# A seven-product step for three of eight k pairs in the last two gate chunks, with sums of weights built in place

## The chip, the cores and the metric

The kernel runs on one core of a Trainium2 chip. The metric is the device time of one execution in microseconds (us). Each time below that has a colon in its window is counted from the start of the profiled execution.

## What is computed

One layer of a hybrid trunk on 256 tokens, width 2048, in float32. The parts that matter here:

```python
gates = sigmoid(h @ w_gate + b_gate).reshape(b, s, 3, d)      # w_gate: 2048 x 6144
merged = gates[:, :, 0] * ya + gates[:, :, 1] * yb + gates[:, :, 2] * yc
x = x + merged @ w_o                                          # 2048 x 2048
h2 = rmsnorm(x, g_mlp)
x = x + square(relu(h2 @ w_up)) @ w_down                      # 2048 x 8192, 8192 x 2048
```

Before that stand an input projection and three short token mixers that give ya, yb and yc; after it a last RMSNorm.

## The kernel before, in words

**Products.** Every weight matrix is read once, in slabs of 1 MB (a tile `raw` of 128 x 2048 values). To keep float32's accuracy with TensorE's float32r operands, each operand is split in a high part and a rest: ScalarE (ACT) writes `hi`, a rounding cast of `raw`, and VectorE (DVE) writes `lo = raw - hi`. One product of a 128 x 128 block of activations with a 128 x 512 block of weights is then three matmuls of 512 columns into one accumulator in PSUM: act_hi by hi, act_hi by lo, act_lo by hi.

**Weights in the pipeline.** Class `W` (lines 75 to 121) loads a slab and prepares it. `raw` has three buffers, `hi` and `lo` two each. `next_w` keeps the preparation of one slab ahead of the matmuls of another: slab p is cast into the `hi` buffer that slab p-2 had, so its cast waits until PE has done the last matmul that reads slab p-2.

**Stages.** Up to 197 us the input projection and the mixers. Then six gate chunks of 1024 columns in the order of `BRANCH_TURNS`, each of eight slabs (two k tiles of 128 by 1024 columns, "one k pair"), each followed by its branch's projection of two or three slabs (`gate`, `branch`, lines 526 to 552). Then the output projection, and four rounds q of an up projection (16 slabs) and a down projection of two chunks c (8 slabs each).

**The seven-product step.** `down_folded` (line 644) already uses it, for seven of the eight down chunks. A slab of two k tiles, two token tiles and two column blocks takes 8 products, 24 matmuls. In the four k pairs of `FOLD` it takes 7 products, 21 matmuls: four sums of activations (`sact`) are made once a round, and four sums of weight blocks for each slab (`W.sums`, line 105). The sums go through a tile `t` of their own: three DVE additions into `t` (lines 110 to 112), then casts `th` and rests `tl` in two halves (lines 116 and 117), then `hi` and `lo` of the three raw blocks that are used as they are (the same lines, 128 x 1536). `th` and `tl` have one buffer. Some products go to one output alone (`dx`), four are shared between outputs and gather in `mb` and `ma`.

```python
nc.vector.tensor_add(t[:, 0:2, :], v[:, 0:3:2, :], v[:, 3:4, :].to_broadcast([P, 2, 512]))
nc.vector.tensor_add(t[:, 2, :], t[:, 1, :], v[:, 0, :])
nc.vector.tensor_add(t[:, 3, :], t[:, 2, :], v[:, 1, :])
```

**Order.** Each engine works through its own list in the order that a scheduler wrote when the program was built, and waits at an instruction until semaphores of the other engines allow it. Within a chunk the scheduler may move matmuls among neighbours.

Names used below: slabs are numbered as they are loaded. Slabs 126 to 133 are the first down chunk of the first round (127, 129, 131, 133 folded), 134 to 141 the second. A sum's tiles bear the number of the slab plus one (`th132` belongs to slab 131).

Of the kernel before, what the change touches and what calls it, by code (L numbers as in the profile page):

```python
# [25 lines left out]
FOLD = (1, 3, 5, 7)  # L26
BRANCH_TURNS = ((2, 0, NCB), (1, 0, NB), (2, 1, NCB), (1, 1, NB), (0, 0, NA), (0, 1, NA))
# [19 lines left out]
def hybrid_trunk(ctx: ExitStack, tc: tile.TileContext, xw_d, gmix_d, xtok_d, wst, wtok, wbr, par_d, wpool_d, bgate_d, gfin_d, out_d):  # L47
# [37 lines left out]
    class W:  # L85
# [19 lines left out]
        def sums(self):  # L105
            v, hi, lo = four(self.raw), four(self.hi), four(self.lo)
            t = pools["fold"].tile([P, 4, 512], F32, name=f"t{serial[0]}", tag="t")
            self.thi = pools["fold"].tile([P, 4, 512], F32R, name=f"th{serial[0]}", tag="th")
            self.tlo = pools["fold"].tile([P, 4, 512], F32R, name=f"tl{serial[0]}", tag="tl")
            nc.vector.tensor_add(t[:, 0:2, :], v[:, 0:3:2, :], v[:, 3:4, :].to_broadcast([P, 2, 512]))  # L110
            nc.vector.tensor_add(t[:, 2, :], t[:, 1, :], v[:, 0, :])
            nc.vector.tensor_add(t[:, 3, :], t[:, 2, :], v[:, 1, :])
            for h, l, r in ((self.thi[:, 0:2, :], self.tlo[:, 0:2, :], t[:, 0:2, :]),
                            (self.thi[:, 2:4, :], self.tlo[:, 2:4, :], t[:, 2:4, :]),
                            (hi[:, 0:3, :], lo[:, 0:3, :], v[:, 0:3, :])):
                fg[1] = nc.scalar.copy(h, r)  # L116
                fg[0] = nc.vector.tensor_sub(l, r, h.bitcast(F32))  # L117
# [398 lines left out]


# [3 lines left out]
    gt = gstack.enter_context(tc.tile_pool(name="gt", bufs=2))  # L521
    acc = gp.tile([P, 2, D], F32, name="acc")
    mstack = ExitStack()
    home = [None]
# [16 lines left out]
    def branch(c, ks, gs, name, n, first=False):  # L541
        banks = fresh_banks(1024, name)
        gemm_tok(yact, banks, 1024, ks, n=n)
        for h in range(2):
# [9 lines left out]
    def merged_channels(c):  # L554
        tp = ps_pair(f"tm{c}").rearrange("p a b -> p (a b)").rearrange("p (j s) -> p j s", s=S)
# [4 lines left out]
        split(home[0][:, 4 * c:4 * c + 4, :], tp)  # L560

    SPAN = {2: list(range(NA + NB, KT)), 1: list(range(NA, NA + NB)), 0: list(range(NA))}
    for b, c, nk in BRANCH_TURNS:
        if b == 0 and c == 0:
# [3 lines left out]
            mp = mstack.enter_context(tc.tile_pool(name="mp", bufs=1, side="right"))  # L568
            home[0] = mp.tile([P, KT, 2 * S], F32R, name="merged")
        turn = {1: lambda: merged_channels(0), 2: lambda: merged_channels(1)} if (b, c) == (0, 1) else None  # L570
        gs = gate(b, c, 4, turn)
        branch(c, SPAN[b], gs, f"y{b}_{c}", 4, first=b == 2)
    merged = home[0]
# [298 lines left out]
```

## Time and profile before

| | |
|---|---|
| median of three runs | 1347.83 us (1347.45 to 1348.12) |
| the profiled execution | 1347.23 us |
| its span, first to last instruction | 1345.3 us |
| PE busy | 1332.8 us, 99% of the span |
| DVE busy | 1009.5 us, 75% |
| ACT busy | 657.6 us, 49% |
| HBM read | 264.71 MB, 198 GB/s over the span |

The profile is of one execution on the chip. Its page gives busy time by engine, the span in 40 slices, and groups of instructions by source line; the trace behind it can be asked for the instructions of a stretch in order of time (a timeline), for busy times in chosen stretches, and for what ended an engine's idle time. Busy time of PE counts overlapping matmuls once, so PE can read as busy all the time; the rate at which matmuls start tells how fast it goes.

### The profile page before, as it was taken

How to read it: one execution, taken by the hardware profiler on the slowest of the kernel's cores; microseconds unless marked ns; L12 is line 12 of the kernel's file. 1: busy time of each engine (PE TensorE's matmuls, PEld its weight loads, DVE VectorE, ACT ScalarE, POOL GpSimd, SP SyncE). 2: the span in 40 equal slices, each digit the busy share in tenths (PEclk: the TensorE clock that was granted, in tenths of full speed). 3: DMA queues.
4: the chain of work that ended last, by engine and by line, in shares of the span. 5: the costliest groups of instructions: out<-in, count | busy, mean ns of one | idle time of the engine just before them, and what ended most of it. 6: DMA issues, size and time to landing. Idle time of an engine off the chain costs nothing.

```text
span 1345.3 us, 16492 instructions
## 1 busy us (share of the span) xinstructions
PE 1332.8 (99%) x6610; PEld 1127.1 (84%) x6610; DVE 1009.5 (75%) x1267; ACT 657.6 (49%) x796; POOL 21.7 (2%) x47
## 2 busy tenths in 40 slices
PE   9999999999999999999999999999999999999997
PEld 8888888888888888888888888888788888888885
DVE  6779888879766465555668996679876799777966
ACT  7545443434454344345445564455544455444544
POOL 0000000000000000000000000000110001100010
PEclk9999999999999999999999999999999999999999
DMA  9655555656556565565455555555775557755682
GB/s 372 221 188 188 188 188 191 211 201 210 197 185 208 197 212 176 197 241 188 157 191 199 204 204 202 188 189 190 227 239 184 192 199 222 236 189 188 214 255 94
DMA packets 42557, 273.11 MB, mean 203 GB/s; under 512 B 4848, under 2 KB 4976, under 8 KB 11888
## 3 DMA queue, kind: packets, MB, share of 16 engines
q1 hardware_dynamic: 38736, 263.67, 56.2%
q0 software_dynamic: 2880, 5.24, 2.2%
q10 hardware_dynamic: 864, 3.15, 0.6%
q8 instruction: 51, 0.84, 0.2%
q14 instruction: 26, 0.21, 0.0%
HBM read 264.71 MB, written 2.10 MB: 198 GB/s over the span
## 4 chain that ended last, share of the span: by engine, by line
PE 91%; DVE 4%; DMA 3%; issue 1%; ACT 0%; SPq 0%; POOLq 0%; POOL 0%; DVEq 0%; ACTq 0%
PE u L124 17%; PE u L127 9%; PE g L511 6%; PE g L510 6%; PE g L512 6%; PE dx L641 4%; PE dx L640 4%; PE dx L642 4%; PE zc L124 3%; PE o L511 2%; PE o L510 2%; PE o L512 2%; PE za L124 2%; DMA raw<-wtok 2%; PE y L511 2%; PE y L510 2%
## 5 line engine op out<-in xcount | busy, mean ns | idle before, releaser
L120 ACT CAST hi<-raw 128x1024 fp32r<-128x1024 f32 x420 | 423.6, 1050 | 434.6 <-PE g L512 134.4
L121 DVE TENSOR_TENSOR lo<-raw,hi 128x1024 fp32r<-128x1024 f32 x420 | 502.0, 1220 | 178.4 <-ACT hi L120 178.3
L124 PE MATMUL u<-hact,hi 128*128 128x512 f32 x1024 | 245.4, 391 | 0.0
L124 PEld LDWEIGHTS u<-hact,hi 128*128 128x128 f32 x1024 | 187.8, 188 | 36.9 <-ACT ps L685 0.4
L510 PE MATMUL g<-hi,hact 128*128 128x512 f32 x384 | 149.9, 390 | 0.0
L512 PE MATMUL g<-hi,hact 128*128 128x512 f32 x384 | 149.4, 389 | 0.0
L511 PE MATMUL g<-lo,hact 128*128 128x512 f32 x384 | 149.4, 389 | 0.0
L127 PEld LDWEIGHTS u<-hact,lo 128*128 128x128 f32 x1024 | 131.4, 191 | 5.1
L127 PE MATMUL u<-hact,lo 128*128 128x256 f32 x1024 | 133.0, 283 | 0.0
L641 PE MATMUL dx<-lo,yact 128*128 128x512 f32 x252 | 98.8, 392 | 0.2 <-DVE lo L121 0.2
L640 PE MATMUL dx<-hi,yact 128*128 128x512 f32 x252 | 98.8, 392 | 0.0
L642 PE MATMUL dx<-hi,yact 128*128 128x512 f32 x252 | 98.4, 391 | 0.0
L329 DVE SCALAR_TENSOR_TENSOR va<-upad,par,va 128x256 f32<-128x256 f32 x180 | 86.8, 482 | 3.4
L510 PEld LDWEIGHTS g<-hi,hact 128*128 128x128 f32 x384 | 72.1, 188 | 15.0
L512 PEld LDWEIGHTS g<-hi,hact 128*128 128x128 f32 x384 | 72.1, 188 | 15.0
L511 PEld LDWEIGHTS g<-lo,hact 128*128 128x128 f32 x384 | 72.1, 188 | 14.8
L116 ACT CAST th<-t 128x1024 fp32r<-128x1024 f32 x56 | 57.5, 1052 | 33.9 <-PE dx L642 15.9
L117 DVE TENSOR_TENSOR tl<-t,th 128x1024 fp32r<-128x1024 f32 x56 | 67.0, 1221 | 8.1 <-ACT th L116 8.1
L192 DVE TENSOR_TENSOR zs_u<-u,cr_u 128x512 f32<-128x512 f32 x32 | 22.1, 692 | 60.6 <-ACT cr_u L190 60.6
L190 ACT COPY cr_u<-u 128x512 f32<-128x512 f32 x32 | 18.8, 588 | 90.6 <-PE u L124 83.4
L640 PEld LDWEIGHTS dx<-hi,yact 128*128 128x128 f32 x252 | 47.3, 188 | 11.4 <-ACT ps L685 0.4
L641 PEld LDWEIGHTS dx<-lo,yact 128*128 128x128 f32 x252 | 47.3, 188 | 10.4 <-DVE lo L121 0.6
(213 smaller groups left out, 1893.1 us busy)
## 6 DMA issues: line engine op xcount, KB each, us to landing
raw<-wtok SPq DMA_DIRECT2D x128, 1024.0 KB, 4.9
raw<-wst SPq DMA_DIRECT2D x93, 1024.0 KB, 4.9
raw<-wbr SPq DMA_DIRECT2D x16, 1024.0 KB, 4.8
xw<-xw SPq DMA_DIRECT2D x7, 768.0 KB, 8.4
macc<-ps POOLq DMA_DIRECT2D x20, 256.0 KB, 7.5
bias<-bgate SPq DMA_DIRECT2D x6, 512.0 KB, 3.6
xt<-xtok SPq DMA_DIRECT2D x8, 256.0 KB, 9.0
xres<-xtok ACTq DMA_DIRECT2D x1, 2048.0 KB, 9.2
```

What stands on the lines that cost most here:

```text
L117: fg[0] = nc.vector.tensor_sub(l, r, h.bitcast(F32))
L120: fg[1] = nc.scalar.copy(self.hi[:, ks], self.raw[:, ks])
L121: fg[0] = nc.vector.tensor_sub(self.lo[:, ks], self.raw[:, ks], self.hi[:, ks].bitcast(F32))
L124: nc.tensor.matmul(ps, w.hi[:, k, :], act[:, ak, :], start=start, stop=stop)
L127: nc.tensor.matmul(ps[:, S:2 * S], w.lo[:, k, :], act[:, ak, 0:S], start=False, stop=False)
L329: nc.vector.scalar_tensor_tensor(va[:, i, :], upad[:, i, k:k + S], pcol(C_WDW + i * KA + k), va[:, i, :], ALU.mult, ALU.add)
L510: nc.tensor.matmul(banks[t][:, c, :], left, hi[:, i, cols], start=first, stop=False)
L511: nc.tensor.matmul(banks[t][:, c, :], left, lo[:, i, cols], start=False, stop=False)
L512: nc.tensor.matmul(banks[t][:, c, :], rest, hi[:, i, cols], start=False, stop=last)
L640: nc.tensor.matmul(ps, left[0], right[0], start=start, stop=False)
L641: nc.tensor.matmul(ps, left[0], right[1], start=False, stop=False)
L642: nc.tensor.matmul(ps, left[1], right[0], start=False, stop=stop)
```

## The change

Four things change together.

1. The gate chunks of branch 0 (the last two, `gate_folded`) use the seven-product step in k pairs 3, 5 and 7 (`GFOLD`). Their activation sums `gsact` are made during an earlier gate chunk. The shared products are taken apart after the chunk, partly beside the branch's matmuls.
2. `W.sums`, for gates and down chunks alike, drops the tile `t`. It first casts `hi` and takes `lo` of three raw blocks, then adds in place over `raw`, then casts `th` and takes `tl`.
3. The merged activations lie in two tiles of half the size. The transposes of the first two quarters use the PSUM tiles `mb` and `ma` of the second folded gate chunk, ahead of their products.
4. The order of the blocks in a folded slab and of its products is another, and `gfin` has a tile of its own.

```diff
+GFOLD = (3, 5, 7)
...
         def sums(self):
             v, hi, lo = four(self.raw), four(self.hi), four(self.lo)
-            t = pools["fold"].tile([P, 4, 512], F32, name=f"t{serial[0]}", tag="t")
...
-            nc.vector.tensor_add(t[:, 0:2, :], v[:, 0:3:2, :], v[:, 3:4, :].to_broadcast([P, 2, 512]))
-            nc.vector.tensor_add(t[:, 2, :], t[:, 1, :], v[:, 0, :])
-            nc.vector.tensor_add(t[:, 3, :], t[:, 2, :], v[:, 1, :])
-            for h, l, r in ((self.thi[:, 0:2, :], self.tlo[:, 0:2, :], t[:, 0:2, :]),
-                            (self.thi[:, 2:4, :], self.tlo[:, 2:4, :], t[:, 2:4, :]),
-                            (hi[:, 0:3, :], lo[:, 0:3, :], v[:, 0:3, :])):
-                fg[1] = nc.scalar.copy(h, r)
-                fg[0] = nc.vector.tensor_sub(l, r, h.bitcast(F32))
+            fg[1] = nc.scalar.copy(hi[:, 0:3, :], v[:, 0:3, :])
+            nc.vector.tensor_sub(lo[:, 0:3, :], v[:, 0:3, :], hi[:, 0:3, :].bitcast(F32))
+            nc.vector.tensor_add(v[:, 0:4:3, :], v[:, 0:2, :], v[:, 3:4, :].to_broadcast([P, 2, 512]))
+            nc.vector.tensor_add(v[:, 1, :], v[:, 1, :], v[:, 0, :])
+            nc.vector.tensor_add(v[:, 2, :], v[:, 2, :], v[:, 1, :])
+            for ks in (slice(0, 4, 3), slice(1, 3)):
+                fg[1] = nc.scalar.copy(self.thi[:, ks, :], v[:, ks, :])
+                fg[0] = nc.vector.tensor_sub(self.tlo[:, ks, :], v[:, ks, :], self.thi[:, ks, :].bitcast(F32))
...
-        stream += [(wtok[next(tok)], KT) for i in range(8)]
+        stream += [(wtok[next(tok)], KT, 1, turn[0] == 0 and i in GFOLD) for i in range(8)]
...
+    def folded_products(av, sums, pairs, name, between=None):
...
+                own = [(xs[0][:, 0, :], a12, b21), (xs[0][:, 1, :], s4, b22), (xs[1][:, 0, :], a22, t4)]
+                shared = [(mb[:, 1, :], s1, t1), (mb[:, 0, :], s3, t3), (ma[:, 1, :], s2, t2), (ma[:, 0, :], a11, b11)]
+                if last:
+                    for ps, left, right in own:
+                        mm3(ps, left, right, False, True)
+                for ps, left, right in shared:
+                    mm3(ps, left, right, first, last)
+                if not last:
+                    for ps, left, right in own:
+                        mm3(ps, left, right)
...
+    def gate_folded(c, between):
...
+        xs, mb, ma = folded_products(hact, gsact, GFOLD, f"g{c}", between)
...
+        for t in range(2):
+            nc.scalar.copy(gs[t], xs[t])
...
+        nc.scalar.copy(m5, mb[:, 1, :])
+        nc.scalar.copy(p1, ma[:, 0, :])
+        def out(t, h, m):
+            g = gs[t][:, h, :]
+            nc.vector.tensor_add(g, g, m)
+            nc.vector.scalar_tensor_tensor(g, g, rtok[:, t:t + 1], bias[:, 512 * h:512 * h + 512], ALU.mult, ALU.add)
+            nc.scalar.activation(g, g, AF.Sigmoid)
+        bg.extend([lambda: nc.vector.tensor_sub(u, p1, ma[:, 1, :]), lambda: nc.vector.tensor_sub(v, u, mb[:, 0, :]),
+                   lambda: out(0, 0, p1), lambda: nc.vector.tensor_sub(u, m5, u), lambda: out(1, 0, v),
+                   lambda: out(0, 1, u), lambda: nc.vector.tensor_sub(v, m5, v), lambda: out(1, 1, v)])
...
+    def gate_sums(i):
+        k = 2 * GFOLD[i]
+        whole = tmp.tile([P, 2, S], F32, name=f"whole{i}", tag="mg")
+        nc.vector.tensor_add(whole, hact[:, k:k + 2, 0:S].bitcast(F32), hact[:, k:k + 2, S:2 * S].bitcast(F32))
...
     for b, c, nk in BRANCH_TURNS:
+        if b == 1 and c == 1:
+            bg.extend([lambda i=i: gate_sums(i) for i in range(len(GFOLD))])
...
-        gs = gate(b, c, 4, turn)
-        branch(c, SPAN[b], gs, f"y{b}_{c}", 4, first=b == 2)
+        gs = gate_folded(c, turn_merged if c else None) if b == 0 else gate(b, c, 4)
+        branch(c, SPAN[b], gs, f"y{b}_{c}", 4, first=b == 2, b0=b == 0)
```

The built program of the changed kernel shows how the lists of the engines come to stand. Three places:

**First place: DVE, preparation of slab 131** (folded; slabs 130 and 132 beside it are plain). Before:

```order
L110 TENSOR_TENSOR t132_5831<-raw131_5827 128x1024 [waits DMAHW7_49,DVE_49]
L111 TENSOR_TENSOR t132_5831<-t132_5831,raw131_5827 128x512 [waits DVE_49]
L112 TENSOR_TENSOR t132_5831<-t132_5831,raw131_5827 128x512 [waits DVE_49]
L121 TENSOR_TENSOR lo130_5800<-raw130_5798,hi130_5799 128x1024 [waits DMAHW6_49,Activation_49]
L121 TENSOR_TENSOR lo130_5800<-raw130_5798,hi130_5799 128x1024 [waits Activation_49]
L117 TENSOR_TENSOR tl132_5833<-t132_5831,th132_5832 128x1024 [waits Activation_49] x2
L117 TENSOR_TENSOR lo131_5829<-raw131_5827,hi131_5828 128x1536 [waits Activation_49]
```

With the change:

```order
L111 TENSOR_TENSOR lo131_5922<-raw131_5920,hi131_5921 128x1536 [waits DMAHW0_49,Activation_49]
L112 TENSOR_TENSOR raw131_5920<-raw131_5920 128x2x512 [waits DVE_49]
L121 TENSOR_TENSOR lo132_5961<-raw132_5959,hi132_5960 128x1024 [waits DMAHW1_49,Activation_49]
L113 TENSOR_TENSOR raw131_5920<-raw131_5920 128x512 [waits DVE_49]
L121 TENSOR_TENSOR lo132_5961<-raw132_5959,hi132_5960 128x1024 [waits Activation_49]
L114 TENSOR_TENSOR raw131_5920<-raw131_5920 128x512 [waits DVE_49]
L117 TENSOR_TENSOR tl132_5925<-raw131_5920,th132_5924 128x2x512 [waits Activation_49]
L117 TENSOR_TENSOR tl132_5925<-raw131_5920,th132_5924 128x1024 [waits Activation_49]
```

Before, the sums come first, as soon as the load has landed, and `lo` last. With the change `lo` comes first, the sums wait for it, and both halves of the next plain slab's `lo` (132, where it was 130's) stand among the additions and ahead of `tl`.

**The same place on ACT.** Before:

```order
L120 CAST hi130_5799<-raw130_5798 128x1024 [waits DMAHW6_49,PE_49,Activation_49]
L120 CAST hi130_5799<-raw130_5798 128x1024
L116 CAST th132_5832<-t132_5831 128x1024 [waits DVE_49,PE_49,Activation_49]
L116 CAST th132_5832<-t132_5831 128x1024 [waits DVE_49]
L116 CAST hi131_5828<-raw131_5827 128x1536 [waits DMAHW7_49,PE_49]
```

With the change:

```order
L110 CAST hi131_5921<-raw131_5920 128x1536 [waits DMAHW0_49,PE_49,Activation_49]
L120 CAST hi132_5960<-raw132_5959 128x1024 [waits DMAHW1_49,PE_49,Activation_49]
L120 CAST hi132_5960<-raw132_5959 128x1024
L116 CAST th132_5924<-raw131_5920 128x2x512 [waits DVE_49,Activation_49]
L116 CAST th132_5924<-raw131_5920 128x1024 [waits DVE_49]
```

The cast of the folded slab's own blocks has moved from last to first, and the two casts of the next plain slab 132 stand ahead of both casts of sums.

**Second place: PE, folded slab 131.** Before, from the last matmul of slab 130:

```order
L642 MATMUL dx0_0_1_5686<-hi130_5799,yact_89 128x512
L640 MATMUL mb0_0_5687<-th132_5832,sact_4920 128x512 [waits Activation_49]
L641 MATMUL mb0_0_5687<-tl132_5833,sact_4920 128x512 [waits DVE_49]
L642 MATMUL mb0_0_5687<-th132_5832,sact_4920 128x512
L640 MATMUL mb0_0_5687<-th132_5832,sact_4920 128x512
L641 MATMUL mb0_0_5687<-tl132_5833,sact_4920 128x512
L642 MATMUL mb0_0_5687<-th132_5832,sact_4920 128x512
L640 MATMUL ma0_0_5688<-th132_5832,sact_4920 128x512 [waits Activation_49]
L641 MATMUL ma0_0_5688<-tl132_5833,sact_4920 128x512 [waits DVE_49]
L642 MATMUL ma0_0_5688<-th132_5832,sact_4920 128x512
L640 MATMUL ma0_0_5688<-hi131_5828,yact_89 128x512 [waits Activation_49]
L641 MATMUL ma0_0_5688<-lo131_5829,yact_89 128x512 [waits DVE_49]
```

With the change, from the fifth matmul of slab 131:

```order
L519 MATMUL dx0_0_0_5780<-lo131_5922,sact_5015 128x512
L520 MATMUL dx0_0_0_5780<-hi131_5921,sact_5015 128x512
L518 MATMUL dx0_0_0_5780<-hi132_5960,yact_89 128x512 [waits Activation_49]
L519 MATMUL dx0_0_0_5780<-lo132_5961,yact_89 128x512 [waits DVE_49]
L520 MATMUL dx0_0_0_5780<-hi132_5960,yact_89 128x512
L518 MATMUL dx0_0_0_5780<-hi132_5960,yact_89 128x512
L518 MATMUL mb0_0_5782<-th132_5924,sact_5015 128x512 [waits Activation_49]
L519 MATMUL dx0_0_0_5780<-lo132_5961,yact_89 128x512
L520 MATMUL dx0_0_0_5780<-hi132_5960,yact_89 128x512
L518 MATMUL dx0_0_0_5780<-hi132_5960,yact_89 128x512
L519 MATMUL dx0_0_0_5780<-lo132_5961,yact_89 128x512 [waits DVE_49]
L520 MATMUL dx0_0_0_5780<-hi132_5960,yact_89 128x512
```

Before, slab 131 runs as a block, sums first. With the change the products of slab 131's own blocks come first, and then matmuls of slab 132 stand among those of slab 131, each new operand with a wait.

**Third place: PE, the last folded slab of the chunk, 133.** Before, from the last matmul of slab 132:

```order
L642 MATMUL dx0_0_1_5686<-hi132_5868,yact_89 128x512
L640 MATMUL dx0_0_1_5686<-th134_5901,yact_89 128x512 [waits Activation_49]
L641 MATMUL dx0_0_1_5686<-tl134_5902,yact_89 128x512 [waits DVE_49]
L642 MATMUL dx0_0_1_5686<-th134_5901,yact_89 128x512
L640 MATMUL dx0_0_0_5685<-hi133_5897,yact_89 128x512 [waits Activation_49]
L641 MATMUL dx0_0_0_5685<-lo133_5898,yact_89 128x512 [waits DVE_49]
```

With the change, from the fifth matmul of slab 133:

```order
L519 MATMUL dx0_0_0_5780<-lo133_5990,sact_5015 128x512
L520 MATMUL dx0_0_0_5780<-hi133_5989,sact_5015 128x512
L518 MATMUL mb0_0_5782<-th134_5992,sact_5015 128x512 [waits Activation_49]
L518 MATMUL dx0_0_1_5781<-th134_5992,yact_89 128x512 [waits Activation_49]
L519 MATMUL mb0_0_5782<-tl134_5993,sact_5015 128x512 [waits DVE_49]
L520 MATMUL mb0_0_5782<-th134_5992,sact_5015 128x512
L518 MATMUL mb0_0_5782<-th134_5992,sact_5015 128x512
L519 MATMUL mb0_0_5782<-tl134_5993,sact_5015 128x512
L520 MATMUL mb0_0_5782<-th134_5992,sact_5015 128x512
L518 MATMUL ma0_0_5783<-th134_5992,sact_5015 128x512
L519 MATMUL dx0_0_1_5781<-tl134_5993,yact_89 128x512 [waits DVE_49]
```

Before, slab 133 begins with a sum's product. With the change, two matmuls that read the two halves of `th134` stand behind six matmuls of the slab's own blocks, with nothing of another slab between them.

In the second chunk of each round and in the two gate chunks the lists read differently in one respect: ACT casts the first half of the sums ahead of the next plain slab's first half, and DVE makes all three additions and the first `tl` ahead of the next plain slab's `lo`. The order of three additions behind `lo` is the same in all 34 folded slabs (28 in down chunks, 6 in gates).

## Rows read from the trace of the kernel before

**Rows 1.** The page: busy time and instructions; DMA issues, KB each, us to landing
```profile
PE 1332.8 (99%) x6610; PEld 1127.1 (84%) x6610; DVE 1009.5 (75%) x1267; ACT 657.6 (49%) x796; POOL 21.7 (2%) x47
...
raw<-wtok SPq DMA_DIRECT2D x128, 1024.0 KB, 4.9
```

**Rows 2.** Busy time of each engine (and instructions) in four stretches, us from the start
```profile
core 0: us, PE busy (x) PEld busy (x) DVE busy (x) ACT busy (x) POOL busy (x), PEclk, DMA share, GB/s
448.00:476.00 28.00, 28.00 (x125) 23.21 (x124) 14.46 (x14) 12.20 (x14) 0.00 (x0) 1.00 0.61 207
733.00:775.00 42.00, 42.00 (x184) 34.12 (x183) 39.56 (x43) 23.09 (x24) 0.00 (x0) 1.00 0.58 200
1326.00:1330.00 4.00, 3.63 (x15) 2.34 (x13) 2.23 (x3) 0.00 (x0) 0.00 (x0) 1.00 0.00 0
1336.00:1345.00 9.00, 0.31 (x2) 0.00 (x0) 2.55 (x6) 2.06 (x4) 0.55 (x1) 0.70 0.44 164
```

**Rows 3.** Groups by line and shape: count, busy us, mean ns, idle before
```profile
L121 DVE TENSOR_TENSOR lo<-raw,hi 128x1024 fp32r<-128x1024 f32 x420 | 502.0, 1220 | 178.4 <-ACT hi L120 178.3
L120 ACT CAST hi<-raw 128x1024 fp32r<-128x1024 f32 x420 | 423.6, 1050 | 434.6 <-PE g L512 134.4 <-issue 113.5 <-PE dx L642 70.4
...
L117 DVE TENSOR_TENSOR tl<-t,th 128x1024 fp32r<-128x1024 f32 x56 | 67.0, 1221 | 8.1 <-ACT th L116 8.1
L116 ACT CAST th<-t 128x1024 fp32r<-128x1024 f32 x56 | 57.5, 1052 | 33.9 <-PE dx L642 15.9 <-issue 13.5 <-DVE t L112 4.5
...
L117 DVE TENSOR_TENSOR lo<-raw,hi 128x1536 fp32r<-128x1536 f32 x28 | 49.2, 1757 | 2.1 <-ACT hi L116 2.1
...
L116 ACT CAST hi<-raw 128x1536 fp32r<-128x1536 f32 x28 | 41.5, 1482 | 2.4 <-PE dx L642 2.4
```

**Rows 4.** PE's timeline, first and 97th matmul of the gate stage: start, length
```profile
197.64 0.39 PE L510 MATMUL g<-hi,hact 128*128 128x512 f32 x1
...
219.41 0.39 PE L510 MATMUL g<-hi,hact 128*128 128x512 f32 x1
```

**Rows 5.** PE's timeline in folded slab 131 of the first down chunk
```profile
759.69 0.40 PE L642 MATMUL mb<-th,sact 128*128 128x512 f32 x1
...
762.48 0.39 PE L642 MATMUL dx<-th,yact 128*128 128x512 f32 x1
...
763.88 0.39 PE L642 MATMUL dx<-hi,sact 128*128 128x512 f32 x1
```

**Rows 6.** ACT's timeline while slabs 131 and 132 run
```profile
762.95 2.00 ACT L116 CAST th<-t 128x1024 fp32r<-128x1024 f32 x2 [1.51 <-issue]
764.85 1.48 ACT L116 CAST hi<-raw 128x1536 fp32r<-128x1536 f32 x1
```

**Rows 7.** DVE's timeline in the same stretch
```profile
764.03 2.36 DVE L117 TENSOR_TENSOR tl<-t,th 128x1024 fp32r<-128x1024 f32 x2 [1.16 <-ACT th L116]
766.36 1.76 DVE L117 TENSOR_TENSOR lo<-raw,hi 128x1536 fp32r<-128x1536 f32 x1
768.04 1.22 DVE L110 TENSOR_TENSOR t<-raw 128x1024 f32<-128x1024 f32 x1
769.29 0.69 DVE L111 TENSOR_TENSOR t<-t,raw 128x512 f32<-128x512 f32 x1
770.02 0.69 DVE L112 TENSOR_TENSOR t<-t,raw 128x512 f32<-128x512 f32 x1
770.63 0.74 DVE L727 SCALAR_TENSOR_TENSOR xres<-dx,stat,xres 128x512 f32<-128x512 f32 x1
```

**Rows 8.** PE's timeline where folded slab 133 begins
```profile
769.82 0.39 PE L641 MATMUL dx<-tl,yact 128*128 128x512 f32 x1
...
770.51 0.39 PE L641 MATMUL dx<-lo,yact 128*128 128x512 f32 x1
```

**Rows 9.** PE's timeline in the last chunk, round its longest wait
```profile
1329.30 0.39 PE L512 MATMUL d<-hi,yact 128*128 128x512 f32 x1
1330.54 0.50 PE L510 MATMUL d<-hi,yact 128*128 128x512 f32 x1 [0.84 <-DVE xres L727]
```

More of the change, by code (lines that the diff above doesn't have):

```diff
@@ L515, in gemm_tok, with mm3, act @@
             pump(n)
+    def mm3(ps, left, right, start=False, stop=False):
+        nc.tensor.matmul(ps, left[0], right[0], start=start, stop=False)
+        nc.tensor.matmul(ps, left[0], right[1], start=False, stop=False)
+        nc.tensor.matmul(ps, left[1], right[0], start=False, stop=stop)
+    def folded_products(av, sums, pairs, name, between=None):
+        xs = [ps_pair(f"dx{name}_{t}") for t in range(2)]
+        mb, ma = ps_pair(f"mb{name}"), ps_pair(f"ma{name}")
+        def act(k, t):
+            return av[:, k, t * P:(t + 1) * P], av[:, k, S + t * P:S + (t + 1) * P]
+        for p in range(8):
+            w = next_w()
+            hi, lo = four(w.hi), four(w.lo)
+            if p in pairs:
+                i = pairs.index(p)
+                a11, a12, a22 = act(2 * p, 0), act(2 * p + 1, 0), act(2 * p + 1, 1)
+                s1, s2, s3, s4 = ((sums[:, i, 0, n, :], sums[:, i, 1, n, :]) for n in range(4))
+                b11, b22, b21 = ((hi[:, n, :], lo[:, n, :]) for n in range(3))
+                t1, t2, t4, t3 = ((w.thi[:, n, :], w.tlo[:, n, :]) for n in range(4))
+                first, last = i == 0, i == len(pairs) - 1
+                own = [(xs[0][:, 0, :], a12, b21), (xs[0][:, 1, :], s4, b22), (xs[1][:, 0, :], a22, t4)]
[8 more added lines that the diff above has]
+                        mm3(ps, left, right)
+            else:
+                for k in range(2):
+                    for t in range(2):
+                        for h in range(2):
+                            mm3(xs[t][:, h, :], act(2 * p + k, t), (hi[:, 2 * k + h, :], lo[:, 2 * k + h, :]),
+                                p == 0 and k == 0, p == pairs[-1] - 1 and k == 1 and t == h == 1)
+            if between:
+                between(p, mb, ma)
+        return xs, mb, ma
@@ L539, in gate, with branch @@
         return gs
-    def branch(c, ks, gs, name, n, first=False):
+    def branch(c, ks, gs, name, n, first=False, b0=False):
         banks = fresh_banks(1024, name)
         gemm_tok(yact, banks, 1024, ks, n=n)
+        if b0:
+            pump(len(bg))
         for h in range(2):
@@ L835 @@
     for b, c, nk in BRANCH_TURNS:
[L836 removed]
+        wtok += slabs(w_gate[:, b * D + 1024 * c:b * D + 1024 * c + 1024], (1024,), GFOLD if b == 0 else ())
         wbr += slabs(w_out[b][:, 1024 * c:1024 * c + 1024], (1024,))
```

97 lines of the change are left out of this document (41 added, 56 removed).

## The prediction

> **What bounds the kernel now.** I read the page first. PE is busy 99% of the span, DVE 75% [rows 1]. Busy time says little of pace, so I then took PE's timeline: from its first to its 97th matmul of the gate stage 21.77 us pass, 96 steps of 0.2268 us each [rows 4]. In folded slab 131 the 18 steps from 759.69 to 763.88 take 4.19 us, 0.2328 each [rows 5]. PE goes without a pause through gates and down chunks: where no matmul waits, time is the number of matmuls times these steps. Next the busy times by stretch. In the gates DVE works 14.46 of 28 us, in the first down chunk 39.56 of 42 us, while PE starts 184 matmuls, 0.228 us each [rows 2]. So DVE there is nearly as full as PE, and what keeps PE from waiting is that DVE works ahead. How far ahead, the timelines tell: the rests of the sums `tl` of slab 133 start at 764.03 and are both done at 766.39; `lo` follows at 766.36 and is done at 768.12 [rows 7]. PE's first matmul on `tl` of slab 133 starts at 769.82, the first on its `lo` at 770.51 [rows 8]. That lead, 3.4 and 2.4 us, is what the change spends.
>
> **What it saves.** Each of six folded gate slabs loses 3 matmuls: 18 x 0.2268 = 4.1 us. The 126 matmuls that stay in them step at 0.2328 instead of 0.2268: 0.8 us back. **Saved: 3.3 us.**
>
> **What the new order of the sums costs.** Durations [rows 3]: a cast of 1024 takes 1.05 us, of 1536 1.48; a DVE rest of 1024 takes 1.22, of 1536 1.76. Steps [rows 6, 7]: an ACT cast starts 0.95 after the one before; a DVE instruction of 1024 lets the next start 1.14 later, one of 512 0.61 (770.02 to 770.63), and an addition that needs the one before starts 1.25 after one of 1024 and 0.73 after one of 512. Hand-over: the last matmul on `th` of slab 131 starts at 762.48 and takes 0.39, and the next `th` cast starts at 762.95 [rows 5, 6], so 0.47 after a matmul's start; DVE starts at 764.03, 0.03 after that cast's end [rows 6, 7], and I take 0.03 for every other hand-over. In-place additions on two far blocks aren't in this trace. They have the size of line 110's (1.22 at 768.04); two additions of 512 would take 1.38 [rows 7]. I take 1.22; the difference is 0.16 a slab, 5 us at most in all 34.
>
> Before, the additions needed only the load, and ran before PE let go of any buffer. Now they stand behind `lo`, `lo` behind `hi`, and `hi` behind PE's last matmul on slab p-2. I walk through **slab 131 of a first chunk**, in the order shown, with time 0 where the last matmul of slab 130 starts.
> - `hi131` needs the last matmul on `hi129`, 15 steps of 0.23 earlier: it starts at -2.98 and ends at -1.50. `lo131` runs -1.47 to 0.29, the first addition 0.32 to 1.54.
> - `hi132` needs slab 130 done: its halves run 0.47 to 1.52 and 1.42 to 2.47. DVE's order then gives `lo132` first half 1.55 to 2.77, second addition 2.69, `lo132` second half 3.30 to 4.52, third addition 4.44 to 5.13.
> - The first `th` ends at 3.42, the second (it needs the third addition) at 6.21; `tl` ends at 6.27 and 7.46.
> - PE: the 8th matmul (the first on `lo132`) could start at 1.84 and gets its operand at 2.80: 0.96 lost. The 15th (second half of `lo132`) loses 0.14, the 20th (second `th`) 0.54. The others find theirs ready. **1.64 us lost**, and since all starts from what PE frees, no lead builds up: slab 129 is alike.
> - First folded slab of the chunk (127): between `lo` and the additions stand the split and sums of the last activations; the same walk gives 1.2 before the first `th` and 0.8 before the second: 2.0.
> - **Last folded slab (133)**: the same chain, but only six matmuls stand before the first `th` (could start at 1.61, ready 3.45: 1.84 lost) and one more before the second (3.68, ready 6.24: 2.56 lost). A DVE addition to `xres` delays the second `tl` to 8.08, 0.26 more. 4.66 together.
>
> A first chunk loses 2.0 + 2 x 1.64 + 4.66 = 9.9 us; there are four: **39.8 us**.
>
> **Second chunks**: ACT casts `th` before the next `hi`, and DVE adds all three before the next `lo`. The `hi` cast starts 21 steps before time 0, at -4.36; `lo` ends at -1.09, the additions at 1.61, the first `th` at 1.24, the next slab's `hi` at 2.19, the first `tl` at 2.75. The 5th, 8th and 9th matmul wait 0.12, 0.26 and 0.33: 0.7 us. The last folded slab has its first `tl` in the 8th place (0.94) and the second in the 15th (0.67): 1.6. The first, behind a first chunk's end, loses 1.6 by the same steps. 4.6 a chunk, three of them: **13.9 us**.
>
> **Gate chunks** have the order of second chunks: 0.7 and 1.6 for their second and third folded slab. The first: 0.2 in one chunk; in the other two rests of 1.22 for the merged halves stand between `lo` and the additions, 1.1. At each branch's end some 20 DVE instructions of 0.7 us (taking the products apart, gates, `acc`) and 6 rests meet in three slabs, 21 us of work in 16.3 of PE, so the next slab's `lo` is some 0.8 late. Sum 2.5 + 3.4 + 1.6: **7.5 us**.
>
> **What I cost at nothing.** The activations' sums for the gates (some 18 short DVE instructions) run in a gate chunk where DVE is half idle [rows 2]; without that cover, some 8 us. The copies of PSUM on ACT, 1.05 each, end before the branch's first matmuls need the banks by the same walk (5.1 against 6.7). The transposes are as many as before. SP's list is as long, but a folded slab's `raw` is free only after its last `tl`: 7.46 in the walk. The load takes 4.9 [rows 1], and the slab that gets this buffer is cast some 13 us later or more in first chunks; in second ones a plain slab needs it by 11.5 and it was freed at 5.03, 1.5 us to spare.
>
> **Sum**: -3.3 + 39.8 + 13.9 + 7.5 = +57.9. The profiled execution took 1347.2, 1.9 more than its span and 0.6 under the median of the runs: **1405**.
>
> **Rivals.**
> - *Faster: the waits don't come.* Then 3.3 us remain: 1344. It needs operands ready in the order in which the scheduler set PE's list: the chain would have to be shorter by 2.6 us before the last folded slab of a first chunk and by about 1 elsewhere, so it decides at the hand-over of the `hi` buffer; if `hi` didn't wait for PE, DVE's 9.3 us of work would fit the 10.4 of a pair. For it: DVE is idle for part of each pair. Against: `hi` has two buffers. If waits of about 3 us remained, gain and loss would cancel, to within 0.2% (about what a measurement of this kernel can tell from no change).
> - *A part of the waits.* The folded slabs in mid-chunk recover their lead, only the last of a chunk and the gates lose: 4 x 4.7 + 3 x 1.6 + 3.2 = 26.8, less 3.3: 1371. For it: first slabs do start from a plain one that left DVE time. Against: every walk starts from a PE event.
> - *The clock falls too.* In the last folded slab of a first chunk PE starts one matmul between 1.38 and 6.24. The longest pause so far, 1.24 us from one start to the next at 1329.30 [rows 9], left the granted clock at 1.00; after PE's end it reads 0.70 on average over 9 us [rows 2], so it does fall from 2.4 to 1.2 GHz in idleness. If it fell in those four places and a slab of 24 matmuls took twice its 5.5 us, that is 22 more: 1427. The Trainium skill says the same of the direction (TensorE: Matmul & The Clock Gate, "What's actually happening": the throttled clock is the default and activity releases it); no row before has a pause like this, so I can't say whether it suffices.
> - *The change doesn't fold what it says*: the built order shows 18 matmuls fewer in the gates, so I give this nothing.
>
> **How the numbers follow.** All waits as walked 0.72; a part 0.12; clock too 0.08; no waits 0.06; cancelled 0.02. So faster 0.06, within 0.2% 0.02, slower 0.92. The walked case alone runs from 1386 (each wait a third shorter, hand-overs and leads being better than taken) to 1415 (additions of 1.38 and hand-overs worse by 0.1). Up to 1427 it takes in the clock; what lies under 1386 holds 0.2. **Range 1386 to 1427.**
>
> **What would show it.** Right: PE's timeline in first down chunks has pauses of about 1 us at the first matmul on the next slab's `lo`, and of 1.8 and 2.6 us at the two first matmuls on `th` of the last folded slab; chunks of 42 us last 52, second chunks 46, and the gate chunks gain no more than they lose. DVE's idle time is put down to casts, ACT's to PE. Wrong: no idle time of PE at these lines, or pauses in one kind of chunk only.

## The result, and the profile after

The changed kernel takes **1411.24 us** (median of 4 runs, 1410.12 to 1411.92) against 1347.64 of the kernel before on the same chip: ratio 1.0469, 95% interval 1.0457 to 1.0481, slower. The forecast was 1405, range 1386 to 1427. The profiled span is 1408.1 us, 62.8 more than before.

The page of the changed kernel: busy time, the chain that ended last, and three groups (count, busy us, mean ns, idle before and what ended it):

```profile
PE 1356.6 (96%) x6592; PEld 1121.9 (80%) x6592; DVE 1050.2 (75%) x1325; ACT 673.8 (48%) x813; POOL 21.6 (2%) x47
...
PE 76%; DVE 13%; ACT 6%; issue 4%; DMA 0%; SPq 0%; POOLq 0%; POOL 0%; ACTq 0%; DVEq 0%
...
L111 DVE TENSOR_TENSOR lo<-raw,hi 128x1536 fp32r<-128x1536 f32 x34 | 59.8, 1758 | 81.9 <-ACT hi L110 81.9
...
L116 ACT CAST th<-raw 128x1024 fp32r<-128x1024 f32 x68 | 70.8, 1045 | 69.5 <-DVE raw L112 47.4
...
L110 ACT CAST hi<-raw 128x1536 fp32r<-128x1536 f32 x34 | 50.4, 1483 | 82.4 <-PE ma L520 40.2
```

PE has 18 matmuls fewer, as the built order said, and is no longer busy all the time. The three groups read backwards are the new chain: `th` waits for additions, `lo` for the cast `hi`, and `hi` for PE. Before, the same three had idle times of 33.9, 2.1 and 2.4 us [rows 3]; now 69.5, 81.9 and 82.4. No duration has grown: 1758 ns for `lo` and 1045 for `th` are those of before.

PE's timeline gives the time by stage: from the first matmul of a chunk to the first matmul behind the chunk.

| | before, us | after, us | difference | forecast |
|---|---|---|---|---|
| four first down chunks, each | 41.4 | 53.0 | 11.6 | 9.9 |
| three second down chunks, each (mean) | 41.65 | 46.06 | 4.4 | 4.6 |
| gate stage, first gate matmul to the last transpose of the merged activations | 375.43 | 379.15 | 3.7 | 4.2 |

4 x 11.6 + 3 x 4.4 + 3.7 = 63.3, the whole of the 62.8 to within 0.5. So nearly all of the loss lies in the down chunks, where the change saves nothing.

Slab 131 of the changed kernel, the one that the prediction walked through. DVE's timeline (start, length):

```profile
764.76 1.76 DVE L111 TENSOR_TENSOR lo<-raw,hi 128x1536 fp32r<-128x1536 f32 x1 [3.23 <-ACT hi L110]
766.55 1.23 DVE L112 TENSOR_TENSOR raw<-raw 128x1024 f32<-128x1024 f32 x1
767.80 1.23 DVE L121 TENSOR_TENSOR lo<-raw,hi 128x1024 fp32r<-128x1024 f32 x1
768.94 0.69 DVE L113 TENSOR_TENSOR raw<-raw 128x512 f32<-128x512 f32 x1
769.54 1.22 DVE L121 TENSOR_TENSOR lo<-raw,hi 128x1024 fp32r<-128x1024 f32 x1
770.68 0.68 DVE L114 TENSOR_TENSOR raw<-raw 128x512 f32<-128x512 f32 x1
771.28 2.42 DVE L117 TENSOR_TENSOR tl<-raw,th 128x1024 fp32r<-128x1024 f32 x2
```

ACT's in the same stretch:

```profile
763.25 1.48 ACT L110 CAST hi<-raw 128x1536 fp32r<-128x1536 f32 x1 [2.97 <-PE ma L520]
766.71 2.00 ACT L120 CAST hi<-raw 128x1024 fp32r<-128x1024 f32 x2 [1.98 <-PE dx L520]
768.62 1.04 ACT L116 CAST th<-raw 128x1024 fp32r<-128x1024 f32 x1
771.39 1.05 ACT L116 CAST th<-raw 128x1024 fp32r<-128x1024 f32 x1 [1.74 <-DVE raw L114]
```

PE's:

```profile
767.86 0.46 PE L518 MATMUL dx<-hi,yact 128*128 128x512 f32 x1
769.08 0.50 PE L519 MATMUL dx<-lo,yact 128*128 128x512 f32 x1 [0.75 <-DVE lo L121]
769.41 0.39 PE L520 MATMUL dx<-hi,yact 128*128 128x512 f32 x1
...
771.85 0.39 PE L520 MATMUL dx<-hi,yact 128*128 128x512 f32 x1
772.50 0.50 PE L518 MATMUL ma<-th,sact 128*128 128x512 f32 x1 [0.26 <-ACT th L116]
```

The walk's time 0 is here 766.23 (2.98 behind the start of `hi131` at 763.25). It put the first addition at 0.32, the two halves of `lo132` at 1.55 and 3.30, the third addition at 4.44: the rows have 0.32, 1.57, 3.31 and 4.45. PE's 8th matmul starts 1.22 behind the one before it, 0.99 over a step (0.96 forecast); the second `th` costs 0.42 (0.54).

The last folded slab of the chunk, 133, on PE:

```profile
779.76 0.39 PE L520 MATMUL dx<-hi,sact 128*128 128x512 f32 x1
781.83 0.50 PE L518 MATMUL mb<-th,sact 128*128 128x512 f32 x1 [1.68 <-ACT th L116]
784.62 0.50 PE L518 MATMUL dx<-th,yact 128*128 128x512 f32 x1 [2.28 <-ACT th L116]
784.95 0.39 PE L519 MATMUL mb<-tl,sact 128*128 128x512 f32 x1
...
785.66 0.63 PE L519 MATMUL mb<-tl,sact 128*128 128x512 f32 x1
786.09 0.63 PE L520 MATMUL mb<-th,sact 128*128 128x512 f32 x1
```

The steps of 2.07 and 2.79 are 1.84 and 2.56 over one of 0.23: the two terms of the walk to the hundredth. What follows was a rival: from 785.66 matmuls start 0.43 apart and take 0.63. The windows before and at these matmuls (busy time by engine, granted clock, DMA share, GB/s):

```profile
779.00:785.00 6.00, 2.03 (x8) 1.11 (x8) 6.00 (x7) 3.82 (x4) 0.00 (x0) 1.00 0.18 40
785.00:789.00 4.00, 4.00 (x12) 3.15 (x11) 3.04 (x5) 1.07 (x2) 0.00 (x0) 0.57 0.87 301
```

The granted clock falls to 0.57 on average over 4 us: 1.2 GHz for most of it. It does so in all four first chunks, for 6 to 8 matmuls, 0.20 each: 1.4 to 1.6 us, 6 in all.

### The profile page after: what moved, and what is told of

Read it like the earlier page. It is cut to its first block, busy times and chain, and to the rows that moved or that the text cites. A ratio compares the mean times of both kernels' runs of the same rounds, so it can differ in the third digit from the quotient of the medians.

```text
span 1408.1 us, 16542 instructions
## 1 busy us (share of the span) xinstructions
PE 1356.6 (96%) x6592; PEld 1121.9 (80%) x6592; DVE 1050.2 (75%) x1325; ACT 673.8 (48%) x813; POOL 21.6 (2%) x47
## 3 DMA queue, kind: packets, MB, share of 16 engines
q1 hardware_dynamic: 38736, 263.67, 53.3%
## 4 chain that ended last, share of the span: by engine, by line
PE 76%; DVE 13%; ACT 6%; issue 4%; DMA 0%; SPq 0%; POOLq 0%; POOL 0%; ACTq 0%; DVEq 0%
PE u L124 17%; PE u L127 9%; PE g L511 4%; PE g L512 4%; PE g L510 4%; DVE lo L121 4%; PE zc L124 3%; DVE lo L111 3%; ACT hi L110 2%; PE o L512 2%; PE o L511 2%; PE o L510 2%; PE za L124 2%; PE y L510 2%; PE y L512 2%
## 5 line engine op out<-in xcount | busy, mean ns | idle before, releaser
L121 DVE TENSOR_TENSOR lo<-raw,hi 128x1024 fp32r<-128x1024 f32 x408 | 490.2, 1220 | 131.1 <-ACT hi L120 130.9
L120 ACT CAST hi<-raw 128x1024 fp32r<-128x1024 f32 x408 | 413.2, 1049 | 342.8 <-issue 114.0
L111 DVE TENSOR_TENSOR lo<-raw,hi 128x1536 fp32r<-128x1536 f32 x34 | 59.8, 1758 | 81.9 <-ACT hi L110 81.9
L116 ACT CAST th<-raw 128x1024 fp32r<-128x1024 f32 x68 | 70.8, 1045 | 69.5 <-DVE raw L112 47.4
L511 PE MATMUL g<-lo,hact 128*128 128x512 f32 x256 | 99.7, 390 | 1.0 <-DVE lo L121 1.0
L510 PE MATMUL g<-hi,hact 128*128 128x512 f32 x256 | 99.7, 390 | 0.0
L512 PE MATMUL g<-hi,hact 128*128 128x512 f32 x256 | 99.6, 389 | 0.0
L110 ACT CAST hi<-raw 128x1536 fp32r<-128x1536 f32 x34 | 50.4, 1483 | 82.4 <-PE ma L520 40.2
L117 DVE TENSOR_TENSOR tl<-raw,th 128x1024 fp32r<-128x1024 f32 x68 | 82.5, 1219 | 0.0
L511 PEld LDWEIGHTS g<-lo,hact 128*128 128x128 f32 x256 | 48.1, 188 | 11.4 <-DVE lo L121 1.4
```

What stands on the lines that cost most here:

```text
L111: nc.vector.tensor_sub(lo[:, 0:3, :], v[:, 0:3, :], hi[:, 0:3, :].bitcast(F32))
L120: fg[1] = nc.scalar.copy(self.hi[:, ks], self.raw[:, ks])
L121: fg[0] = nc.vector.tensor_sub(self.lo[:, ks], self.raw[:, ks], self.hi[:, ks].bitcast(F32))
L510: nc.tensor.matmul(banks[t][:, c, :], left, hi[:, i, cols], start=first, stop=False)
L511: nc.tensor.matmul(banks[t][:, c, :], left, lo[:, i, cols], start=False, stop=False)
L512: nc.tensor.matmul(banks[t][:, c, :], rest, hi[:, i, cols], start=False, stop=last)
```

## The experiments

**1 to 4: where the loss comes from.** The theory is the prediction's: the sums stand behind `lo`, `lo` behind `hi`, `hi` behind PE, and the gates matter little. Rivals: the folded gates cost it; writing over the raw block costs it.

*1. Gates as before, sums in place in the down chunks.*

```diff
-GFOLD = (3, 5, 7)
+GFOLD = ()
...
-        gs = gate_folded(c, turn_merged if c else None) if b == 0 else gate(b, c, 4)
+        gs = gate(b, c, 4, {1: lambda: merged_channels(0), 2: lambda: merged_channels(1)} if (b, c) == (0, 1) else None)
...
```

> The changed kernel with the gate chunks as before (24 matmuls in every slab, no gate sums); the in-place sums stay in the down chunks. Theory (the sums behind lo, lo behind the hi cast, hi behind PE, cost in the down chunks; the gates cost little): the gates' waits in the trace of the changed kernel add up to 4.4 us, one wait beside the gate sums to 1.1, some 0.1 us behind each of ten waits to 1.1, 6.6 together, against 3.3 saved; so 1411.2 + 3.3 - 6.6 = 1408, and the pauses of 2.07 and 2.79 us in the last folded slabs of first down chunks stay. Rival (folding the gates, taking the products apart and the split merged tile cost most): near the time before, 1348 to 1360.

Measured: 1408.12, ratio 1.0443 (1.0429 to 1.0457); its gate stage takes 375.43, as before, and its first down chunks 53.0 to 54.1 (54.1 in one of four, where the clock was low for twice as long as in the others). The loss doesn't need the folded gates.

*2. In place in the gates only; in down chunks a tile of their own, additions first.*

```diff
+            if "sum" not in pools:
+                fg[1] = nc.scalar.copy(hi[:, 0:3, :], v[:, 0:3, :])
...
+                return
+            t = pools["sum"]()
+            nc.vector.tensor_add(t[:, 0:4:3, :], v[:, 0:2, :], v[:, 3:4, :].to_broadcast([P, 2, 512]))
...
```

> The changed kernel with the sums of the down chunks in a tile of their own again, additions first; in place only in the six gate slabs. Theory: 1347.6 - 3.3 + 6.6 = 1351, between 1348 and 1354; no pause over 0.5 us in the down chunks, granted clock 1.00. Rival (gates cost most): above 1390.

Measured: 1351.08, ratio 1.0021 (1.0012 to 1.0030); down chunks 41.3 and 41.4. The two parts are apart: 60.1 and 3.0 us over the kernel before on the same chip, where the table has 59.6 for the down chunks and 3.7 for the gates. Experiments 2 and 3 also keep the code's new order of blocks and products (part 4 of the change) and the merged activations in two tiles (part 3), so neither of these is what costs the time.

*3. Folded gates kept, sums in a tile of their own everywhere, additions first.* In the gates half of the tile lies in two small ones.

```diff
-            nc.vector.tensor_add(v[:, 0:4:3, :], v[:, 0:2, :], v[:, 3:4, :].to_broadcast([P, 2, 512]))
-            nc.vector.tensor_add(v[:, 1, :], v[:, 1, :], v[:, 0, :])
-            nc.vector.tensor_add(v[:, 2, :], v[:, 2, :], v[:, 1, :])
+            nc.vector.tensor_add(ta, v[:, 0:2, :], v[:, 3:4, :].to_broadcast([P, 2, 512]))
+            nc.vector.tensor_add(tb[:, 0, :], v[:, 1, :], ta[:, 0, :])
+            nc.vector.tensor_add(tc_[:, 1 if tb is tc_ else 0, :], v[:, 2, :], tb[:, 0, :])
...
+            fg[1] = nc.scalar.copy(hi[:, 0:3, :], v[:, 0:3, :])
+            fg[0] = nc.vector.tensor_sub(lo[:, 0:3, :], v[:, 0:3, :], hi[:, 0:3, :].bitcast(F32))
```

> Folded gates kept, sums in a tile of their own everywhere, additions first in the code. Theory: the 3.3 us saved remain, less the wait of 1.1 beside the gate sums and some 0.3 at the ends of the gate chunks: 1345.5, between 1344 and 1348. Rival (gates cost most): as before that edit or worse, above 1390. Rival (the gates' own waits come from taking the products apart, not from the order of the sums): 1350.

Measured: 1345.16, ratio 0.9978 (0.9969 to 0.9987): 0.2% under the kernel before, with an interval that leaves out 1. The gate stage takes 373.61, 1.8 less than before, so folding the gates does pay; the way the sums were built took it and much more. Another 1.3 lies in the down chunks (41.31 and 41.36 each, before 41.43 and 41.65), so not in the folding.

*4. The same tiles, but the additions held behind `lo`.*

```diff
+            with tc.issue_after(fg[0].ins):
...
+                nc.vector.tensor_add(ta, v[:, 0:2, :], v[:, 3:4, :].to_broadcast([P, 2, 512]))
...
```

> Sums in a tile of their own everywhere, but hi and lo first and the additions held behind lo in DVE's list, as they stand in the changed kernel. Theory in its form that the order alone costs: as the changed kernel, 1411, between 1400 and 1420, with the same two pauses of about 2 and 2.8 us in last folded slabs. Rival (writing over the raw block is what is slow: the strided addition on two far blocks, a raw buffer held to the last tl, loads that start later): back near 1346 to 1355.

Measured: 1399.38, ratio 1.0377 (1.0361 to 1.0393). It lies 0.6 under the range that I gave the theory, and far from the rival's. The order alone costs 54 of the 66 us between experiment 3 and the changed kernel, with nothing written over. The two steps in the last folded slab are 2.08 and 1.55:

```profile
776.34 0.39 PE L523 MATMUL dx<-hi,sact 128*128 128x512 f32 x1
778.42 0.50 PE L521 MATMUL mb<-th,sact 128*128 128x512 f32 x1 [1.70 <-ACT th L119]
779.97 0.50 PE L521 MATMUL dx<-th,yact 128*128 128x512 f32 x1 [1.04 <-ACT th L119]
```

The first is the changed kernel's; the second is 1.24 shorter. In this kernel the scheduler put the second addition ahead of the first half of the next slab's `lo`, and the third addition ahead of its second half; in the changed kernel each stands behind that half. So 12 us were open: other lists, or writing in place.

**5: the same lists, in place.** Two edges bring the in-place kernel's lists to those of experiment 4; in first down chunks they are then the same on DVE, ACT and PE. `behind` holds the second addition and the first `tl` of the slab ahead (in the gates the second `tl`, twice).

```diff
+                if behind:
+                    with tc.issue_after(behind.pop(0).ins):
+                        self.prep(ks)
...
```

> The changed kernel, in place everywhere, with its lists brought near those of the run with tiles of their own and the additions behind lo (1399.4): on DVE, in down chunks, the next plain slab's first lo behind the second addition and its second lo behind the first tl; in the gates both behind the second tl. In first down chunks the lists of DVE, ACT and PE are then the same in both kernels, and only the place of the sums differs. Theory (order alone): first down chunks of 50.8 to 52.8 us as in that run, where the changed kernel took 53.0; the whole near 1400 to 1404, since the gates' casts are still other ones. Rival (writing over the raw block costs something of its own): first down chunks stay at 53 or more, the whole at 1407 or above.

Measured: 1403.78, ratio 1.0410 (1.0393 to 1.0428); first down chunks 51.2 to 53.3 (50.8 to 52.8 in experiment 4). The 53.3 is a chunk in which the clock fell for 13 matmuls. In the first round the waits over 0.1 us of that chunk add up to 8.3 us, in experiment 4 to 7.9, in the changed kernel to 9.0. The 0.4 between the first two goes with one dependency, 0.11 to 0.14 in each of slabs 129, 131 and 133; in the second round, where the clock stays up in both kernels, the chunks differ by as much (51.19 and 50.84). DVE's timeline of slab 133, first of experiment 4:

```profile
773.48 1.76 DVE L111 TENSOR_TENSOR lo<-raw,hi 128x1536 fp32r<-128x1536 f32 x1 [3.30 <-ACT hi L110]
775.15 1.22 DVE L114 TENSOR_TENSOR t<-raw 128x1024 f32<-128x1024 f32 x1
```

Then of this one:

```profile
774.70 1.76 DVE L117 TENSOR_TENSOR lo<-raw,hi 128x1536 fp32r<-128x1536 f32 x1 [3.28 <-ACT hi L116]
776.50 1.23 DVE L118 TENSOR_TENSOR raw<-raw 128x1024 f32<-128x1024 f32 x1
```

Here an addition that writes over what `lo` reads starts 1.80 behind it, one into another tile 1.67. The addition on two far blocks takes 1.23, not the 1.38 that I feared. Of the 12 us the two edges give back 7.5. The 4.4 left are that dependency, the gates, whose casts of sums are other ones in experiment 4 (375.75 us for the stage here, 374.66 there), and the clock; I did not part them further.

**6: take PE's release away.** In place as in the changed kernel, but two folded slabs of each down chunk have `hi` and `lo` in a third pair of buffers.

```diff
-            self.hi = whi.tile([P, KT, P], F32R, name=f"hi{n}", tag="hi")
+            third = folded and "sact" in pools and n % 4 == 3
+            ph, pl = (pools["fold"], pools["fold"]) if third else (whi, wlo)
+            self.hi = ph.tile([P, 12 if third else KT, P], F32R, name=f"hi{n}", tag="hi")
...
```

> The changed kernel, in place everywhere, but in the down chunks the first and third folded slab of each chunk take hi and lo from a third pair of buffers, so that no cast of a folded slab needs what PE freed just before: slab 131 waits for no matmul, slab 133 for slab 130. Theory (the chain hi, lo, additions, th, tl is long, but it is late only because it starts at PE's release of the hi buffer): the waits of the down chunks go, the gates keep theirs: 1347.6 - 3.3 + 6.6 = 1351, between 1349 and 1362. Rival (working in place is slow in itself, or the chain is too long for the time of two slabs wherever it starts): above 1390.

Measured: 1351.45, ratio 1.0033 (1.0021 to 1.0045); down chunks 41.3 and 41.4 to 41.9, without a wait in the first round. The gate stage keeps its 379.1. The chain has the same operations as in the changed kernel, and DVE is as full as before. Its busy times over 42 us of a first down chunk, beside 39.56 us of DVE in [rows 2], and the group of `lo`:

```profile
737.00:779.00 42.00, 42.00 (x184) 34.26 (x183) 39.85 (x43) 24.64 (x26) 0.00 (x0) 1.00 0.57 200
```

```profile
L113 DVE TENSOR_TENSOR lo<-raw,hi 128x1536 fp32r<-128x1536 f32 x34 | 59.8, 1758 | 31.0 <-ACT hi L112 30.3
```

DVE's idle time before `lo` is 31.0 instead of 81.9. So neither the work nor the length of the chain costs time by itself here; that the chain starts where PE lets a buffer go does.

**7: the two long waits.** One edit: the preparation of the plain slab that opens a second chunk is held behind the last `tl` of the folded slab ahead of it (its casts behind the last `th`).

```diff
+            if "macc" in pools and pools["macc"](n):
+                with tc.issue_after(fg[0].ins), tc.issue_after(fg[1].ins):
+                    self.prep(slice(0, nk // 2))
...
```

> The changed kernel, with one edit: the preparation of the plain slab that opens a second down chunk is held behind the last tl of the folded slab before it. Theory: the additions of that slab no longer stand among the next slab's lo; first th at 2.62 instead of 3.45 and second at 4.07 instead of 6.24 in the walk of slab 133, so the two long waits of 1.84 and 2.56 become some 1.0 and 1.2: 2.2 less in each of four chunks; and if it is pauses of this length that let the clock fall, the eight steps of 0.427 us go too, 1.6 in each: 1411.2 - 8.8 - 6.4 = 1396. If the clock falls all the same: 1402. Rival (the next slab's lo comes late in its place and takes all of it): 1409 to 1413.

Measured: 1402.94, ratio 1.0406 (1.0392 to 1.0421), 7 us over my 1396 and 1 over the 1402 that I gave for a clock that falls all the same. PE in the last folded slab of the first round:

```profile
781.24 0.50 PE L523 MATMUL mb<-th,sact 128*128 128x512 f32 x1 [0.98 <-ACT th L121]
783.15 0.55 PE L523 MATMUL dx<-th,yact 128*128 128x512 f32 x1 [1.41 <-ACT th L121]
783.50 0.63 PE L524 MATMUL mb<-tl,sact 128*128 128x512 f32 x1
```

And of the last round:

```profile
1339.95 0.50 PE L523 MATMUL mb<-th,sact 128*128 128x512 f32 x1 [0.97 <-ACT th L121]
1341.86 0.51 PE L523 MATMUL dx<-th,yact 128*128 128x512 f32 x1 [1.41 <-ACT th L121]
1342.21 0.39 PE L524 MATMUL mb<-tl,sact 128*128 128x512 f32 x1
```

The waits shrink to 1.13 and 1.68 (walked: 1.0 and 1.2), 1.6 less in each chunk instead of 2.2. And the clock still falls in the first two rounds (0.63 a matmul), while after the same two pauses it stays up in the last two (0.39). The mean clock of the four runs of this kernel reads 0.996, 0.994, 0.996 and 0.994, so the falls seem to differ from run to run as well. Whether the clock falls isn't set by the lengths of these pauses alone; what else sets it stays open.

**8: fill the pauses.** The changed kernel with 18 matmuls by a block of zeros in the last folded slab of first chunks; they add nothing to the sums.

```diff
+                        for n in range(4):
+                            z = nc.tensor.matmul(mb[:, 1, :], pools["zero"], b22[0], start=False, stop=False)
...
+                        for n in range(10):
+                            z = nc.tensor.matmul(mb[:, 1, :], pools["zero"], b22[0], start=False, stop=False)
```

> The changed kernel with 18 further matmuls by a block of zeros in the last folded slab of each first down chunk: 8 ahead of the first matmul on th, 10 between the first and the second, so that PE works through most of the two pauses; the waits themselves stay. Theory (PE's idle time is what lets the clock fall there): the eight steps of 0.427 us become 0.23, 1.6 in each of four places, and the step of 0.11 behind a wait goes in some: 1411.2 - 6.4 = 1405, granted clock 1.00 there. Rival (the slow steps come from the operands, as th and tl just written, or from something else in the slab): 1411 to 1413 with the steps of 0.427 still there.

Measured: 1405.31, ratio 1.0428 (1.0414 to 1.0442), under the changed kernel's interval: faster by 5.9 us **with 72 matmuls more**. PE's timeline, then the window at the matmuls that were slow:

```profile
782.48 0.49 PE L548 MATMUL mb<-th,sact 128*128 128x512 f32 x1
782.81 2.50 PE L551 MATMUL mb<-hi,zero 128*128 128x512 f32 x10
785.25 0.50 PE L518 MATMUL dx<-th,yact 128*128 128x512 f32 x1
785.60 0.39 PE L553 MATMUL mb<-tl,sact 128*128 128x512 f32 x1
...
786.73 0.39 PE L518 MATMUL ma<-th,sact 128*128 128x512 f32 x1
787.10 0.50 PE L519 MATMUL dx<-tl,yact 128*128 128x512 f32 x1
```

```profile
785.00:789.00 4.00, 4.00 (x17) 2.84 (x16) 3.85 (x6) 1.28 (x3) 0.00 (x0) 1.00 0.82 283
```

The operands come as late as in the changed kernel (the second `th` is done 6.21 us behind the last matmul of slab 132, there 6.20), but the clock is 1.00 and the same products step at 0.23. So the slow steps were PE's idleness, not the operands. The Trainium skill has the clock low by default and released by activity (TensorE: Matmul & The Clock Gate, "What's actually happening"); this pair of runs agrees, with 0.57 in the changed kernel and 1.00 here.

**9: the wait that I had not costed.** PE in a gate chunk of experiment 3, and what DVE did there:

```profile
407.14 0.50 PE L513 MATMUL g<-lo,hact 128*128 128x512 f32 x1 [0.97 <-DVE lo L123]
```

```profile
400.63 1.29 DVE L636 TENSOR_TENSOR whole<-hact 128x512 f32<-128x512 f32 x2
...
405.87 1.22 DVE L123 TENSOR_TENSOR lo<-raw,hi 128x1024 fp32r<-128x1024 f32 x1
```

The three activation sums, but for the end of the third, stand in one piece of 5.2 us, from 400.63 to 405.87, ahead of a slab's `lo`. Experiment 3, with the sums handed out one slab at a time:

```diff
-            bg.extend([lambda i=i: gate_sums(i) for i in range(len(GFOLD))])
+            for i in range(len(GFOLD)):
+                bg.extend([lambda i=i: gate_sums(i), None])
```

> Sums in a tile of their own, additions first, and the three activation sums of the gates handed out one slab at a time in the gate chunk that makes them, not within two slabs. Theory (the wait of 1.13 us at 405.8 comes from some 20 short DVE instructions that stand ahead of a slab's lo): that wait goes and nothing takes its place, 1345.2 - 1.2 = 1344. Rival (the wait is the chunk's own): 1345.2.

Measured: 1344.05, ratio 0.9972 (0.9961 to 0.9982). The wait is gone, and `lo` stands among the short instructions:

```profile
402.08 0.68 DVE L636 TENSOR_TENSOR whole<-hact 128x512 f32<-128x512 f32 x1
...
403.42 1.22 DVE L123 TENSOR_TENSOR lo<-raw,hi 128x1024 fp32r<-128x1024 f32 x1
404.55 0.28 DVE L567 TENSOR_TENSOR sa<-whole,sa 128x128 f32<-128x128 f32 x1
```

The gate stage takes 372.30, 3.1 less than before (3.3 forecast for the folding). The intervals of this run and of experiment 3 overlap; the trace parts them, the ratios don't. By its median it is the fastest version here: the gates folded as in the change, the sums in a tile of their own ahead of `lo`, as before.

## Why the prediction was right

It forecast slower by the order of the sums, 1405; the time is 1411, in the range. Step by step:

- **What bounds it**: the lead of 3.4 and 2.4 us that `tl` and `lo` had [rows 7, 8] was what the change spent. Right, and shown by experiment 6: where the chain can start earlier, the same work costs next to nothing in the down chunks.
- **Saved, 3.3**: 3.1 in experiment 9, where nothing else is in its way.
- **Slab 131**: walked 0.96, 0.14, 0.54; the rows have 0.99, nothing, 0.42. Slab 127: 1.2 and 0.8, measured 1.20 and 0.61. Slab 133: 1.84 and 2.56 exactly; the 0.26 behind them doesn't show while the clock is low, and with the clock up, in experiment 8, it is 0.14 (787.10). All waits of a first chunk: 9.9 walked, 9.0 measured.
- **Mis-sized: the first chunks lose 11.6, not 9.9.** Two things that the walk left out. First, the matmul behind every waiting one starts some 0.11 late (0.33 from 769.08 to 769.41), about nine times a chunk, 1 us. The sign of it was in the rows: the matmul that waited in [rows 9] reads 0.50 long, where others read 0.39, and the next starts 0.34 behind it. Second, the clock, 1.6 a chunk, 6 in all. I had it as a rival that excludes the forecast, with a whole slab of 24 matmuls slow: 22 us. It came together with the walked waits, for 6 to 8 matmuls. A cost that any of the cases can carry should have stood in the sum as a term with bounds, not as a case.
- **Second chunks**: 4.6 forecast, 4.4 measured, in part by luck. The waits are 3.9, the late steps behind them 0.8, and the chunks before had some 0.3 of their own over those of experiment 3.
- **Gates**: 7.5 lost forecast, 3.7 + 3.3 = 7.0 by the stage; that is luck in part. The waits within the folded slabs came nearly as walked (4.5 of 4.8), the other parts that I named didn't come. These are the waits at the branch ends (1.6) and the 1.1 behind the rests for the merged halves. The activation sums, costed at nothing beside a half idle DVE, cost 1.1 in one place, and the steps behind waits another 1. "Half idle" is an average over 28 us [rows 2]; the sums stood in one piece.
- **Costed at nothing, and right**: copies, transposes, loads. With the additions early, the folded gates leave no wait of note but that one, and experiment 6 holds every raw block to its last `tl` without a loss in the first round.
- **Rivals**: no waits, and a part of the waits, fell by the table above; the clock rival was a true mechanism of a quarter of its size.
- **The sum**: the waits that were walked came to some 52 us of the 61 forecast, and some 14 that the sum left out (late steps 7, the clock 6, the activation sums 1) made up for it. That 1411 lies so near 1405 is luck in part; that it lies in the range is not, as those waits alone would give 1347.2 - 3.1 + 52 = 1396. The lower end of the range is added up a microsecond too high: with each wait a third shorter, -3.3 + 61.2 x 2/3 = 37.5, which makes 1385.

## What to carry to other kernels

Before an operation is moved behind another to save a buffer, ask what starts the chain: one that starts at a load can run ahead, one that starts at the release of a double buffer can't, and then what it takes beyond the matmuls that PE has in hand counts, though DVE and ACT are idle in between. Walk the built order with row durations from that release: here the two longest waits came out to the hundredth, all the waits of a first chunk to 9.0 of 9.9, and a third buffer took nearly all of those in the down chunks back. Add to every wait of PE the late step behind it, and where two pauses stand close, bounds for the slower clock.

## What was not expected of the hardware

- In the profiled executions the clock fell behind steps of 1.36 and 1.91 us, one behind the other, in two of four places (experiment 7), behind 2.08 and 1.55 in three of four (experiment 4), behind 2.07 and 1.68 in three of four (experiment 5), behind 2.07 and 2.79 in all four; behind a single one of 1.24 in [rows 9] it did not.
- 72 further matmuls made the kernel 5.9 us faster (experiment 8).
- A matmul that waited is followed by a step of 0.33 to 0.34 instead of 0.23, here after nearly every wait, long or short, at the full clock.
